# RWKV-7 trunk: state kept in PSUM and updated on 64x64 quarters, with scores, state and outputs sharing two banks

## The chip, the cores and the metric

The kernel runs on 1 core of one Trainium2 chip. The metric is device time in microseconds (us) of one execution; lower is better. Names: TensorE (PE, weight loads PEld), VectorE (DVE), ScalarE (ACT), GpSimd (POOL), SyncE (SP, which issues most loads).

## The reference, cut to what matters

One layer on 2048 tokens of width 1024, float32: RMSNorm, RWKV-7 time mixing, residual, RMSNorm, squared-ReLU MLP, residual, final RMSNorm. The time mixing has 16 heads of 64 and a 64x64 state per head:

```python
def rwkv7_step(state, inp):
    r_t, w_t, k_t, v_t, a_t, b_t = inp
    sa = jnp.einsum('bhvk,bhk->bhv', state, a_t)
    state = (state * w_t[:, :, None, :]
             + sa[..., None] * b_t[:, :, None, :]
             + v_t[..., None] * k_t[:, :, None, :])
    y = jnp.einsum('bhvk,bhk->bhv', state, r_t)
    return state, y
```

Here a is minus the normalized key direction and b is it times a learned rate. Afterwards y is normalized per head, given a bonus term, gated, and multiplied by an output matrix.

## The kernel before

**Tiling of the recurrence.** The sequence is cut into 4 blocks of 512 tokens, each block into 4 windows of 128 tokens (w = 0 to 15), each window into 4 chunks of 32 tokens (c = 0 to 3). Decays are folded into the factors per window, so within a window the state only gains terms, and the window's total decay is multiplied on at its last chunk. The 16 heads go as 8 even and 8 odd heads (`par` 0 and 1); head p of a parity is written p = 4 hf + k.

**One window**, in the order in which `stage_b` issues it:

- `b_pre` loads the factors (`Le`, `Lo`: those of the even heads on partitions 0 to 63 and of the odd heads on 64 to 127; `Bk`: both), and makes the scores for two chunks at a time: `sce` from `Le` in the PSUM bank tagged `pre`, `sco` from `Lo` in the bank tagged `chain`, by 64x64 matmuls in four positions of the array (line 589). ScalarE copies the part for the solve (line 593), VectorE masks the scores into the other halves of `Le` and `Lo` (line 595).
- `b_solve` inverts the 32x32 unit triangles by forward substitution on VectorE (lines 604 to 612); `b_inv` spreads the inverse into `xbd`.
- `b_chain` issues `b_chunk` four times. A chunk: transposes of `Bk` through `pre` into `ls` (tile `pb`, every second chunk); `pw` (line 652), its copy `ws` (line 655), the pseudo values `pu` = `xbd` times `ws` (line 658), four copies of `pu` into the rows of `suv` (lines 659 to 662), the new state `pS` (lines 665 and 666), and its copies into the state rows of the next `suv` (line 672, or line 670 with the decay at c = 3). `suv` holds, per parity, 64 rows of state, 32 of pseudo values and 32 of v; `ls` holds a 64x64 identity on the state's rows, so that `pS` is the whole state, old plus new.
- `b_y` multiplies the window's outputs y from `Lo`, `Le` and the four `suv` into the banks `y0` and `y1` (line 688).
- `b_fin` normalizes and gates y on VectorE and ScalarE one parity after the other (lines 704 to 722), transposes the result through `y0` or `y1` (tile `pz`, line 726) and copies it to `zt` (line 727). It is called one window late: behind the chain of window w + 1.

**Order around it.** The program's instructions are issued by a list scheduler; the order in which the code issues them is their priority. The recurrence of a block is a generator, `side`, of 80 steps, that the main work draws from at a set rate. From about 676 to 1045 us block 0 runs beside the projections of later blocks (`v_proj`, `g_proj`, matmuls `pv`, `pg`, `pm`); there the loads of the next window are double buffered and its scores come ahead of the chain. From then on `phase_c` computes the output projection (`po`), the MLP (`pu` with lines 90 to 92, `pd`) and the norms of block i while block i + 1 recurs, and draws what is left of the side stage before the next block's output projection (`"complete"`). Its matmuls are splits of float32 into two fp32r parts, three products each (lines 90 to 92); ScalarE makes the first part of each weight tile (line 84), VectorE the rest (line 85). The norms' broadcasts use `y0`.

PSUM has 8 banks: `pre`, `chain`, `y0`, `y1`, and four for the main work's matmuls.

Of the kernel before, what the change touches and what calls it, by code (L numbers as in the profile page):

```python
# [9 lines left out]
F32 = mybir.dt.float32  # L10
F32R = mybir.dt.float32r
AF = mybir.ActivationFunctionType
ALU = mybir.AluOpType
# [4 lines left out]
P = 128  # L18
# [6 lines left out]
NB = T // TB  # L25
# [3 lines left out]
NC = WIN // CH  # L29
# [10 lines left out]
def trunk(ctx: ExitStack, tc, xt, vecs, lnw, lnb, wr, wk, wv, w1a1, w2, a2,  # L40
          g1m, g1t, g2m, g2t, wo, up, down, outT):
    nc = tc.nc
# [456 lines left out]
    start = head(0)  # L499
# [58 lines left out]
    CB = 1  # L558
# [7 lines left out]
    def b_pre(w, r, bp, ps, cfg):  # L566

        i, wd = divmod(w, NWB)
        Le = bp.tile([P, 8, NC, 64], F32, tag="Le", name=f"Le{w}", bufs=cfg["l"])
        Lo = bp.tile([P, 8, NC, 64], F32, tag="Lo", name=f"Lo{w}", bufs=cfg["l"])  # L570
        bk = bp.tile([P, 8, NC, 64], F32, tag="Bk", name=f"Bk{w}", bufs=cfg["l"])
        ec = bp.tile([P, KT], F32, tag="ecw", name=f"ecw{w}", bufs=cfg["l"])
        bon = bp.tile([P, 16], F32, tag="bonw", name=f"bonw{w}", bufs=2)
        nc.sync.dma_start(Le[0:64], d_ar[i][wd, 0:64])
        nc.sync.dma_start(Lo[64:128], d_ar[i][wd, 64:128])
        nc.sync.dma_start(bk, d_bk[i][wd])
        nc.sync.dma_start(ec, d_ec[i][:, :, wd])
        nc.sync.dma_start(bon, d_bon[i][:, wd, :])

        sy = bp.tile([P, 8, NC, 32], F32, tag="sys", name=f"sy{w}")  # L580
        for c in range(0, NC, 2):

            sce = ps.tile([P, 2, 4, 64], F32, tag="pre", name=f"sce{w}_{c}", bufs=cfg["pre"])
            sco = ps.tile([P, 2, 4, 64], F32, tag="chain", name=f"sco{w}_{c}", bufs=CB)
            for e2 in range(2):
                for k in range(4):
                    for (sc, L, rw, hf, cl) in ((sce, Le, 0, 0, 64), (sco, Lo, 64, 0, 0), (sce, Le, 0, 1, 0), (sco, Lo, 64, 1, 64)):
                        p, rr = 4 * hf + k, slice(rw, rw + 64)
                        nc.tensor.matmul(sc[cl:cl + 64, e2, k, :], bk[rr, p, c + e2, :], L[rr, p, c + e2, :],
                                         start=(e2 + k == 0), stop=True, skip_group_check=True, tile_position=(rw, cl))  # L590
            c2 = slice(c, c + 2)
            for n, sc in enumerate((sce, sco)):
                nc.scalar.copy(sy[0:96, 4 * n:4 * n + 4, c2, :].rearrange("s p c t -> s c p t"), sc[0:96, :, :, 0:32])
            for (sc, L, cl, hf, to) in ((sce, Le, 64, 0, 64), (sce, Le, 0, 1, 64), (sco, Lo, 0, 0, 0), (sco, Lo, 64, 1, 0)):
                nc.vector.tensor_tensor(L[to:to + 64, 4 * hf:4 * hf + 4, c2, :].rearrange("s p c t -> s c p t"), sc[cl:cl + 64],
                                        mask[cl:cl + 64].unsqueeze(1).unsqueeze(1).to_broadcast((64, 2, 4, 64)), ALU.mult)
            yield
            yield
        r.Le, r.Lo, r.bk, r.ec, r.bon, r.sy = Le, Lo, bk, ec, bon, sy
# [27 lines left out]
    def b_chunk(w, c, r, bp, ps, cfg):  # L627
# [27 lines left out]
        nc.vector.tensor_copy(ws, pw)  # L655
        pu = ps.tile([P, 4, 64], F32, tag="chain", name=f"pu{w}_{c}", bufs=CB)
        for k in range(4):
            nc.tensor.matmul(pu[:, k, :], xbd[:, k, c, :], ws[:, k, :], start=(k == 0), stop=True, skip_group_check=True)  # L658
        nc.vector.tensor_copy(S[0][64:96, 0:4], pu[64:96])
        nc.vector.tensor_copy(S[0][64:96, 4:8], pu[0:32])  # L660
        nc.scalar.copy(S[1][0:32, 0:4], pu[32:64])
        nc.scalar.copy(S[1][0:32, 4:8], pu[96:128])  # L662
        pS = ps.tile([P, 8, 64], F32, tag="chain", name=f"pS{w}_{c}", bufs=CB)
        for p in range(8):
            nc.tensor.matmul(pS[0:64, p, :], lsc[0][:, p, :], S[0][:, p, :], start=(p == 0), stop=True, skip_group_check=True)  # L665
            nc.tensor.matmul(pS[64:128, p, :], lsc[1][:, p, :], S[1][:, p, :], start=(p == 0), stop=True, skip_group_check=True)
        for par in range(2):
            r = slice(64 * par, 64 * par + 64)
            if c == NC - 1:
                nc.vector.tensor_tensor(Sn[par][r], pS[r], ec[r].unsqueeze(2).to_broadcast((64, 8, 64)), ALU.mult)  # L670
            else:
                nc.scalar.copy(Sn[par][r], pS[r])

    def b_chain(w, r, bp, ps, cfg):

# [4 lines left out]

    def b_y(w, r, ps):

        r.y = []
        for par, L in ((0, r.Le), (1, r.Lo)):
            y = ps.tile([P, 8, 64], F32, tag=f"y{par}", name=f"y{w}_{par}")
            for p in range(8):
                for c in range(NC):
                    nc.tensor.matmul(y[32 * c:32 * c + 32, p, :], L[:, p, c, 32:64], suv[(w * NC + c) % NS][par][:, p, :],
                                     start=(p == 0), stop=True, skip_group_check=True, tile_position=(0, 32 * c))
            r.y.append(y)  # L690

    def b_fin(w, r, bp, ps, cfg):

# [6 lines left out]
        for par, y in enumerate(r.y):  # L700
# [19 lines left out]
            nc.vector.tensor_mul(yc, yc, lnwb[:, cols].rearrange("p (h v) -> p h v", v=64))  # L720
            nc.vector.tensor_add(yc, yc, vb)
            nc.vector.tensor_mul(yc, yc, gb)
            pz = ps.tile([P, 4, P], F32, tag=f"y{par}", name=f"pz{w}_{par}")
            ycf = yc.rearrange("p h v -> p (h v)")
            for k in range(4):
                nc.tensor.transpose(pz[:, k, :], ycf[:, k * P:k * P + P], ident)
# [2 lines left out]

    def stage_b(i, bp, ps, cfg):  # L730
        w0, w1 = i * NWB, (i + 1) * NWB
        r, last = Win(), None
        yield from b_pre(w0, r, bp, ps, cfg)
        yield from b_solve(w0, r, bp)
        for w in range(w0, w1):
            b_inv(w, bp)
            for _ in range(cfg["slack"]):
                yield
            nxt = Win()
            early = cfg["l"] > 1 and w + 1 < w1  # L740
            if early:
                yield from b_pre(w + 1, nxt, bp, ps, cfg)
            yield from b_chain(w, r, bp, ps, cfg)
            if last:
                yield from b_fin(w - 1, last, bp, ps, cfg)
            b_y(w, r, ps)
            if w + 1 < w1:
                if not early:
                    yield from b_pre(w + 1, nxt, bp, ps, cfg)
                yield from b_solve(w + 1, nxt, bp)  # L750
            last, r = r, nxt
        yield from b_fin(w1 - 1, last, bp, ps, cfg)


    p0 = ExitStack()
# [62 lines left out]
    def c_norm(i):  # L818

        h = hs[i]  # L820
        ns = nss.setdefault(i, [])
        pb = norm(h, f"n{i}", cp, psb, "y0", 2)
        rb = cp.tile([P, TB], F32, tag="rb", name=f"nB{i}")
        nc.scalar.copy(rb, pb)
        rbs[i] = rb
        if i > 0:
            for k in range(KT):
                n32 = cp.tile([P, TB], F32, tag="t0", name=f"hn{i}_{k}", bufs=2)
                nc.vector.scalar_tensor_tensor(n32, h[k], vec[:, V_FFN, k:k + 1], rb, ALU.mult, ALU.mult)
                ns.append(split(e, n32, f"hn{i}_{k}"))  # L830
# [30 lines left out]

    def c_sum(i):

        return norm_sum(hs[i], f"f{i}", cp, psb, "y0", 2, 1, i == NB - 1)

    def c_final(i, so):
        h = hs[i]
        pb = norm_rest(so, f"f{i}", cp, psb, "y0")
        rb = cp.tile([P, TB], F32, tag="rb", name=f"fB{i}")
        nc.scalar.copy(rb, pb)  # L870
        for k in range(KT):
# [120 lines left out]
```

## Time and profile before

| | |
|---|---|
| median of 3 runs | 2978.05 us (2973.08 to 2983.74) |
| the profiled execution | 2975.33 us |
| its span, first to last instruction | 2973.6 us |
| mean granted TensorE clock | 0.976 of full speed |

The profile is one execution. A timeline row gives an instruction's start and duration in us, its engine, source line, output and inputs, and shape; a matmul's duration contains its way through the array, so the distance from one start to the next is what a matmul occupies. A float32 matmul of the recurrence is listed as two instructions. Merged rows carry a count (x64). In brackets is the engine's idle time before the instruction and what ended it. A few records of matmuls can be missing.

### The profile page before, as it was taken

Reading aid. Unit: us, or ns where it says so; the run is one execution under the profiler, and the core shown is the slowest. Engines: PE = TensorE matmul, PEld = TensorE weight load, DVE = VectorE, ACT = ScalarE, POOL = GpSimd, SP = SyncE. Lnnn points to the kernel's source line nnn. Section 1 sums busy time; section 2 is a strip of 40 time slices with the busy share of each in tenths; the row PEclk is TensorE's granted clock in tenths of the full one; section 3 lists DMA queues with packets and bytes.
Section 4 is the critical chain, followed back from the end, with each engine's and each line's share of the span. In section 5 each row is a group of like instructions: output and inputs, shape, how many; then the busy total and the mean of one; then the engine's idle time right before and its main releaser. Section 6 shows DMA issues by size and latency. Waiting matters only on the chain.

```text
span 2973.6 us, 49932 instructions
## 1 busy us (share of the span) xinstructions
PE 2809.7 (94%) x19144; PEld 2126.0 (71%) x19144; DVE 2062.6 (69%) x3882; ACT 1423.2 (48%) x2607; POOL 238.2 (8%) x316
## 2 busy tenths in 40 slices
PE   8999999987989989999999999999999999999998
PEld 5766667754555667777777777778777777878886
DVE  5688888867886667678668767865886696544443
ACT  5667666743564243443434454353445435443342
POOL 0102020120010100000012000001200000110000
PEclk9999999998999999999999999999999999999999
DMA  4444454565553533424343333443343342333332
GB/s 132 153 152 163 153 184 160 170 203 188 166 177 125 156 95 94 114 83 122 97 144 110 109 113 88 116 118 118 111 114 107 96 112 83 113 122 97 91 100 78
DMA packets 192542, 373.91 MB, mean 126 GB/s; under 512 B 41136, under 2 KB 41712, under 8 KB 187696
## 3 DMA queue, kind: packets, MB, share of 16 engines
q1 hardware_dynamic: 175216, 305.49, 35.0%
q0 software_dynamic: 17088, 65.24, 5.8%
q8 instruction: 150, 2.46, 0.4%
q14 instruction: 88, 0.72, 0.1%
HBM read 303.32 MB, written 67.32 MB: 125 GB/s over the span
## 4 chain that ended last, share of the span: by engine, by line
PE 46%; DVE 11%; ACT 3%; DMA 3%; issue 2%; POOL 1%; SPq 0%; DVEq 0%; ACTq 0%; POOLq 0%
PE pd L92 6%; PE pd L90 6%; PE pd L91 6%; PE pu L90 5%; PE pu L91 5%; PE pu L92 5%; DVE tmp L611 2%; DVE M L612 2%; PE po L90 2%; PE po L91 2%; PE po L92 2%; PE pS L665 1%; PE pu L658 1%; DMA Le<-d_ar 1%; DVE d_wl L85 1%
## 5 line engine op out<-in xcount | busy, mean ns | idle before, releaser
L92 PE MATMUL pd<-uh,d_wl 128*128 128x512 f32 x1024 | 408.1, 399 | 8.8 <-DVE d_wl L85 8.6
L90 PE MATMUL pd<-uh,d_wh 128*128 128x512 f32 x1024 | 407.1, 398 | 2.4 <-ACT d_wh L84 2.4
L91 PE MATMUL pd<-ul,d_wh 128*128 128x512 f32 x1024 | 402.1, 393 | 0.0
L84 ACT CAST d_wh<-d_w 128x512 fp32r<-128x512 f32 x256 | 158.0, 621 | 353.5 <-PE pd L91 161.4
L84 ACT CAST u_wh<-u_w 128x512 fp32r<-128x512 f32 x256 | 157.8, 620 | 317.7 <-PE pd L91 114.3
L860 DVE TENSOR_TENSOR h<-h,pd 128x512 f32<-128x512 f32 x256 | 174.6, 682 | 154.6 <-PE pd L92 153.8
L85 DVE TENSOR_TENSOR d_wl<-d_w,d_wh 128x512 fp32r<-128x512 f32 x256 | 178.0, 698 | 107.5 <-ACT d_wh L84 97.6
L92 PEld LDWEIGHTS pd<-uh,d_wl 128*128 128x128 f32 x1024 | 192.9, 188 | 61.5 <-DVE d_wl L85 18.7
L85 DVE TENSOR_TENSOR u_wl<-u_w,u_wh 128x512 fp32r<-128x512 f32 x256 | 181.0, 710 | 78.5 <-ACT u_wh L84 69.7
L90 PEld LDWEIGHTS pd<-uh,d_wh 128*128 128x128 f32 x1024 | 193.5, 189 | 42.0 <-ACT d_wh L84 3.2
L91 PEld LDWEIGHTS pd<-ul,d_wh 128*128 128x128 f32 x1024 | 193.0, 189 | 42.3 <-DVE ul L849 0.2
L611 DVE TENSOR_TENSOR tmp<-M 96x30 f32<-96x30 f32 (+14 forms) x480 | 156.9, 327 | 18.9 <-POOL M L605 9.3
L612 DVE TENSOR_TENSOR M<-M,tmp 96x30 f32<-96x30 f32 (+14 forms) x480 | 161.1, 336 | 10.5
L849 DVE TENSOR_TENSOR ul<-rl,uh 128x512 fp32r<-128x512 f32 x128 | 90.2, 705 | 67.9 <-ACT uh L848 67.5
L194 PE MATMUL pv<-v,xv 128*128 128x512 f32 x256 | 124.8, 623 | 11.6 <-DMA v<-in_wv 9.7
L845 ACT ACTIVATE rl<-rl 128x512 f32<-128x512 f32 x128 | 80.9, 632 | 39.8 <-DVE rl L842 37.2
L665 PEld LDWEIGHTS pS<-suv,ls 128*64 128x64 f32 x1024 | 64.6, 138 | 34.0 <-ACT suv L662 29.7
L194 PEld LDWEIGHTS pv<-v,xv 128*128 128x128 f32 x256 | 46.7, 196 | 58.1 <-issue 40.2
L848 ACT CAST uh<-rl 128x512 fp32r<-128x512 f32 x128 | 79.3, 620 | 3.6
L658 PEld LDWEIGHTS pu<-ws,xbd 128*128 128x128 f32 x512 | 64.9, 193 | 22.3 <-DVE ws L655 9.7
L665 PE MATMUL pS<-suv,ls 128*64 128x64 f32 x1024 | 73.7, 225 | 6.5 <-ACT suv L662 6.0
L605 POOL TENSOR_SCALAR_AFFINE_SELECT M<-M 96x1024 f32<-96x1024 f32 x16 | 23.0, 1438 | 700.6 <-DVE M L604 700.6
(711 smaller groups left out, 7074.7 us busy)
## 6 DMA issues: line engine op xcount, KB each, us to landing
u_w<-in_up SPq DMA_DIRECT2D x256, 256.0 KB, 2.7
d_w<-in_down SPq DMA_DIRECT2D x256, 256.0 KB, 2.6
k_w<-in_wk SPq DMA_DIRECT2D x64, 256.0 KB, 2.7
r_w<-in_wr SPq DMA_DIRECT2D x64, 256.0 KB, 2.7
d_ar<-ar POOLq DMA_DIRECT2D x32, 512.0 KB, 3.2
d_bk<-bk POOLq DMA_DIRECT2D x32, 512.0 KB, 3.4
Bk<-d_bk SPq DMA_DIRECT2D x16, 1024.0 KB, 5.0
o_w<-in_wo SPq DMA_DIRECT2D x64, 256.0 KB, 2.9
```

Of the source, the lines that this page charges most:

```text
L84: nc.scalar.copy(hi[0:rows, 0:cols], raw[0:rows, 0:cols])
L85: nc.vector.tensor_tensor(lo[0:rows, 0:cols], raw[0:rows, 0:cols], hi[0:rows, 0:cols], ALU.subtract)
L90: nc.tensor.matmul(out, lhs[0], rhs[0], start=first, stop=False)
L91: nc.tensor.matmul(out, lhs[0], rhs[1], start=False, stop=False)
L92: nc.tensor.matmul(out, lhs[1], rhs[0], start=False, stop=last)
L194: nc.tensor.matmul(pv[tt], xs_[k][:, c], w, start=(k == 0), stop=(k == KT - 1))
L611: nc.vector.tensor_tensor(tv, M[0:96, s + 1:32, s:s + 1].to_broadcast((96, n, s)), M[0:96, s:s + 1, 0:s].to_broadcast((96, n, s)), ALU.mult)
L612: nc.vector.tensor_tensor(M[0:96, s + 1:32, 0:s], M[0:96, s + 1:32, 0:s], tv, ALU.add)
L658: nc.tensor.matmul(pu[:, k, :], xbd[:, k, c, :], ws[:, k, :], start=(k == 0), stop=True, skip_group_check=True)
L665: nc.tensor.matmul(pS[0:64, p, :], lsc[0][:, p, :], S[0][:, p, :], start=(p == 0), stop=True, skip_group_check=True)
L849: nc.vector.tensor_tensor(ul, rl, uh, ALU.subtract)
L860: nc.vector.tensor_add(h[m], h[m], pd)
```

## The change

- The scores `sce` and `sco` become the two halves of one tile of two banks, tag `st`.
- `pu` is multiplied in two column halves of 64 instead of 128 columns at once.
- The state isn't built anew in each chunk: it stays in a tile of two banks (tag `st` again, one per window), which the first chunk writes in full (128 rows, identity included) and chunks 1 to 3 add to, by matmuls over the 64 rows of pseudo values and v alone. Each matmul has a 64x64 position: parity 0 takes rows 64 to 127 of the array and parity 1 rows 0 to 63, parity and head half hf give the column half, and each parity has its own bank.
- The state leaves PSUM in four pieces of 64x256 instead of two of 64x512.
- The two outputs y become one tile of two banks, tag `st`; `pz` and the norms' tiles go to tag `pre`. So `st` holds in turn scores, state, y.
- `b_fin` of window w follows `b_y` of window w directly, ahead of the next window's `b_pre` (in block 0, where that comes early, ahead of the next `b_solve`).

```diff
         for c in range(0, NC, 2):
-            sce = ps.tile([P, 2, 4, 64], F32, tag="pre", name=f"sce{w}_{c}", bufs=cfg["pre"])
-            sco = ps.tile([P, 2, 4, 64], F32, tag="chain", name=f"sco{w}_{c}", bufs=CB)
+            sct = ps.tile([P, 2, 2, 4, 64], F32, tag="st", name=f"sc{w}_{c}")
+            sce, sco = sct[:, 0], sct[:, 1]
...
         for k in range(4):
-            nc.tensor.matmul(pu[:, k, :], xbd[:, k, c, :], ws[:, k, :], start=(k == 0), stop=True, skip_group_check=True)
+            for cl in (0, 64):
+                nc.tensor.matmul(pu[cl:cl + 64, k, :], xbd[:, k, c, cl:cl + 64], ws[:, k, :], start=(k == 0), stop=True,
+                                 skip_group_check=True, tile_position=(0, cl))
...
-        pS = ps.tile([P, 8, 64], F32, tag="chain", name=f"pS{w}_{c}", bufs=CB)
-        for p in range(8):
-            nc.tensor.matmul(pS[0:64, p, :], lsc[0][:, p, :], S[0][:, p, :], start=(p == 0), stop=True, skip_group_check=True)
-            nc.tensor.matmul(pS[64:128, p, :], lsc[1][:, p, :], S[1][:, p, :], start=(p == 0), stop=True, skip_group_check=True)
-        for par in range(2):
-            r = slice(64 * par, 64 * par + 64)
+        if c == 0:
+            r.st = ps.tile([P, 2, 8, 64], F32, tag="st", name=f"st{w}")
+        for k in range(4):
+            for par, hf, cl in ((0, 0, 0), (1, 0, 64), (0, 1, 64), (1, 1, 0)):
+                p = 4 * hf + k
+                r0 = 0 if c == 0 else 64 - 64 * par
+                rw = slice(0, P) if c == 0 else slice(r0, r0 + 64)
+                nc.tensor.matmul(r.st[cl:cl + 64, par, k, :], lsc[par][rw, p, :], S[par][rw, p, :], start=(c == 0 and k == 0), stop=True,
+                                 skip_group_check=True, tile_position=(r0, cl))
+        for par, hf, cl in ((0, 0, 0), (1, 0, 64), (0, 1, 64), (1, 1, 0)):
+            rw = slice(64 * par, 64 * par + 64)
+            ph = slice(4 * hf, 4 * hf + 4)
+            src = r.st[cl:cl + 64, par, 0:4, :]
             if c == NC - 1:
-                nc.vector.tensor_tensor(Sn[par][r], pS[r], ec[r].unsqueeze(2).to_broadcast((64, 8, 64)), ALU.mult)
+                nc.vector.tensor_tensor(Sn[par][rw, ph], src, ec[rw, ph].unsqueeze(2).to_broadcast((64, 4, 64)), ALU.mult)
             else:
-                nc.scalar.copy(Sn[par][r], pS[r])
+                nc.scalar.copy(Sn[par][rw, ph], src)
...
-        r.y = []
+        yt = ps.tile([P, 2, 8, 64], F32, tag="st", name=f"y{w}")
+        r.y = [yt[:, 0], yt[:, 1]]
...
-            pz = ps.tile([P, 4, P], F32, tag=f"y{par}", name=f"pz{w}_{par}")
+            pz = ps.tile([P, 4, P], F32, tag="pre", name=f"pz{w}_{par}")
...
             yield from b_chain(w, r, bp, ps, cfg)
-            if last:
-                yield from b_fin(w - 1, last, bp, ps, cfg)
             b_y(w, r, ps)
+            yield from b_fin(w, r, bp, ps, cfg)
             if w + 1 < w1:
...
-            last, r = r, nxt
-        yield from b_fin(w1 - 1, last, bp, ps, cfg)
+            r = nxt
...
-        pb = norm(h, f"n{i}", cp, psb, "y0", 2)
+        pb = norm(h, f"n{i}", cp, psb, "pre", 2)
```

## Rows read from the trace of the kernel before

**Rows 1.** The page's first part: busy us (share of the span) and instructions.
```profile
PE 2809.7 (94%) x19144; PEld 2126.0 (71%) x19144; DVE 2062.6 (69%) x3882; ACT 1423.2 (48%) x2607; POOL 238.2 (8%) x316
```

**Rows 2.** Busy us of PE, PEld, DVE, ACT, POOL by stretch; clock, DMA, GB/s.
```profile
676.00:1045.00 369.00, 327.66 (x3072) 198.23 (x3071) 280.44 (x595) 173.41 (x338) 39.94 (x62) 0.94 0.52 159
1045.00:2510.00 1465.00, 1409.28 (x11592) 1124.65 (x11593) 1055.44 (x2055) 643.23 (x1235) 69.14 (x70) 0.99 0.37 108
```

**Rows 3.** Waits of TensorE, 1045 to 2510 us: total, times, longest.
```profile
PE pd L92 <- DVE d_wl L85: 8.6, 12, 1.5
```

**Rows 4.** Timeline of TensorE, one chunk: start us, duration us, instruction.
```profile
1320.72 0.40 PE L90 MATMUL pu<-hn_6h,u_wh 128*128 128x512 f32 x1
1321.05 0.24 PE L652 MATMUL pw<-suv,Le 128*32 128x64 f32 x1
...
1321.97 0.39 PE L92 MATMUL pu<-hn_6h,u_wl 128*128 128x512 f32 x1
1322.20 0.40 PE L90 MATMUL pu<-hn_7h,u_wh 128*128 128x512 f32 x1
1322.43 1.00 PE L658 MATMUL pu<-ws,xbd 128*128 128x64 f32 x8
...
1323.56 0.39 PE L92 MATMUL pu<-hn_7h,u_wl 128*128 128x512 f32 x1
...
1324.94 0.40 PE L92 MATMUL pd<-uh,d_wl 128*128 128x512 f32 x1
1325.27 0.27 PE L665 MATMUL pS<-suv,ls 128*64 128x64 f32 x1
...
1326.68 0.40 PE L91 MATMUL pd<-ul,d_wh 128*128 128x512 f32 x1
```

**Rows 5.** Timeline of TensorE, a joined score run; 63 of its instructions left out.
```profile
1121.25 0.39 PE L92 MATMUL pd<-uh,d_wl 128*128 128x512 f32 x1
1121.57 0.27 PE L589 MATMUL sce<-Le,Bk 64*64 64x64 f32 x1
...
1123.01 0.40 PE L91 MATMUL pd<-ul,d_wh 128*128 128x512 f32 x1
```

**Rows 6.** Timeline of TensorE, a pair of score runs apart.
```profile
1238.78 1.15 PE L589 MATMUL sce<-Le,Bk 64*64 64x64 f32 x32 [0.80 <-DMA Le<-d_ar]
...
1242.03 0.40 PE L91 MATMUL pd<-ul,d_wh 128*128 128x512 f32 x1
1242.36 1.15 PE L589 MATMUL sco<-Lo,Bk 64*64 64x64 f32 x32
...
1243.78 0.39 PE L90 MATMUL pd<-uh,d_wh 128*128 128x512 f32 x1
```

**Rows 7.** Groups by line and form: busy us, mean ns, idle before.
```profile
L672 ACT COPY suv<-pS 64x512 f32<-64x512 f32 x96 | 55.7, 581 | 34.3 <-PE pS L666 33.4
...
L647 ACT COPY ls<-pb 64x256 f32<-64x256 f32 x128 | 46.8, 366 | 30.1 <-PE pb L643 22.1 <-PE pS L666 6.0
```

**Rows 8.** Timelines of TensorE and VectorE around y, windows 5 and 7.
```profile
1231.43 1.10 PE L688 MATMUL y<-suv,Le 128*32 128x64 f32 x64
...
1478.29 1.39 DVE L670 TENSOR_TENSOR suv<-pS,ecw 64x512 f32<-64x512 f32 x2 [0.21 <-PE pS L666]
...
1482.93 1.10 PE L688 MATMUL y<-suv,Le 128*32 128x64 f32 x64
...
1487.71 1.10 PE L688 MATMUL y<-suv,Lo 128*32 128x64 f32 x64
...
1499.45 0.69 DVE L715 TENSOR_REDUCE st<-y 128x8 f32<-128x512 f32 x1
```

**Rows 9.** Timelines of ScalarE and TensorE at the end of block 2.
```profile
2003.91 0.59 ACT L727 COPY zt<-pz 128x512 f32<-128x512 f32 x1
...
2013.57 0.59 ACT L727 COPY zt<-pz 128x512 f32<-128x512 f32 x1 [4.05 <-PE pz L726]
...
2018.20 0.40 PE L90 MATMUL po<-z_0h,o_wh 128*128 128x512 f32 x1
```

More of the change, by code (lines that the diff above doesn't have):

```diff
@@ L681, in b_y @@
     def b_y(w, r, ps):
-        r.y = []
+        yt = ps.tile([P, 2, 8, 64], F32, tag="st", name=f"y{w}")
+        r.y = [yt[:, 0], yt[:, 1]]
         for par, L in ((0, r.Le), (1, r.Lo)):
-            y = ps.tile([P, 8, 64], F32, tag=f"y{par}", name=f"y{w}_{par}")
             for p in range(8):
                 for c in range(NC):
-                    nc.tensor.matmul(y[32 * c:32 * c + 32, p, :], L[:, p, c, 32:64], suv[(w * NC + c) % NS][par][:, p, :],
+                    nc.tensor.matmul(r.y[par][32 * c:32 * c + 32, p, :], L[:, p, c, 32:64], suv[(w * NC + c) % NS][par][:, p, :],
                                      start=(p == 0), stop=True, skip_group_check=True, tile_position=(0, 32 * c))
-            r.y.append(y)
     def b_fin(w, r, bp, ps, cfg):
@@ L731, in stage_b @@
         w0, w1 = i * NWB, (i + 1) * NWB
-        r, last = Win(), None
+        r = Win()
         yield from b_pre(w0, r, bp, ps, cfg)
@@ L862, in c_sum @@
     def c_sum(i):
-        return norm_sum(hs[i], f"f{i}", cp, psb, "y0", 2, 1, i == NB - 1)
+        return norm_sum(hs[i], f"f{i}", cp, psb, "pre", 2, 1, i == NB - 1)
     def c_final(i, so):
         h = hs[i]
-        pb = norm_rest(so, f"f{i}", cp, psb, "y0")
+        pb = norm_rest(so, f"f{i}", cp, psb, "pre")
         rb = cp.tile([P, TB], F32, tag="rb", name=f"fB{i}")
```

## The prediction

> **What bounds the kernel now.** I read the page's first part, then a table by stage, then the waits of TensorE, then timelines of single chunks. TensorE is busy for 94% of the span [rows 1], and by stage that is 328 of 369 us in the stretch in which the recurrence of block 0 runs beside value and gate projections (676 to 1045 us), and 1409 of 1465 us where the recurrences of blocks 1 to 3 run beside the output projection and the MLP (1045 to 2510 us) [rows 2]. The rest of the span holds nothing of the change. In the long stretch the largest wait of TensorE for one thing comes to 8.6 us [rows 3]: the recurrence is cheap there in latency, because independent MLP matmuls fill in, and dear in TensorE slots, because each of its instructions displaces one of theirs. So the question is how long a run of recurrence matmuls keeps the MLP stream off TensorE. I price a run by the stream around it: from the last stream matmul before the run to the second one after it, less two stream steps of 0.23 us (1321.97 to 1322.20 in rows 4). That counts what a change of form costs on entering and leaving.
>
> **The state update.** Now it is 16 matmuls a chunk, 128 rows by 64 columns, which the profile lists as 32 instructions: 1324.94 to 1326.68 is 1.74 us, less 0.46 gives 1.28 us [rows 4]. Two column halves start together, so these are 16 steps. After the change 48 of the 64 chunks (those that aren't a window's first) use 64x64 quarters, whose four positions can start together: 8 steps. Quarters stand in the trace already, in the scores. Where all four run, 64 instructions cost 1121.25 to 1123.01, 1.76 less 0.46, 1.30 us [rows 5], for twice as many instructions as the state's. Eight steps are seen in the `pw` run, 32 instructions in four column quarters: 1320.72 to 1321.97, 1.25 less 0.46, 0.79 us [rows 4]. I take 0.79, so 0.49 us saved for each of 48 chunks, 23.5 us: 17.6 in the long stretch (36 chunks), 5.9 in the first (12). The other end is no gain: where only two positions are in flight, 32 quarter instructions cost as much as the state does now (1.29 us, next but one paragraph). I take the upper end because the new order visits the four positions in turn, as the scores in rows 5 do, with each row half on its own bank. A window's first chunk keeps its 16 steps and costs what it does.
>
> **Pseudo values in column halves.** 4 matmuls of 128x128 (8 instructions) cost 1322.20 to 1323.56, 1.36 less 0.46, 0.90 us [rows 4]. In halves they are 16 instructions in pairs, 8 steps, by the `pw` run 0.79 us: 0.11 us saved for each of 64 chunks, 7.0 us (5.3 and 1.8). Ends: if the halves didn't overlap, 16 steps at the state's 1.28 us would lose 0.38 us a chunk, 24 us; the state's own pairs, two halves of 64 columns starting together, are the same form and speak against that.
>
> The stream's step grows from 0.23 to 0.33 us on entering the `pw` and `pS` runs, and stays 0.23 us on entering the full-size `pu` run [rows 4]. The Trainium skill (TensorEngine Tiling (Array Packing), Key Properties) says that changing the tiling mode drains TensorE, which speaks against halving `pu`: the trace agrees by that 0.10 us. By the rule alone, two switches more in 64 chunks would lose about 13 us where I forecast a gain of 7; by the rows, the 0.79 us has both switches in it.
>
> **Scores.** Now the even heads' scores take the bank `pre` and the odd ones `chain`, each issued as its inputs come; after, both stand in one tile, so neither starts before the tile is free. Where they run apart, each 32 instructions cost a full run: 1242.03 to 1243.78, 1.75 less 0.46, 1.29 us [rows 6], so 2.58 us a pair against 1.30 joined. Of the 22 pairs of score runs in the long stretch I count 16 apart, as at 1238.78 and 1242.36. What separates them is the odd heads' load, queued behind the even heads'. After the change the tile is freed by the window's last read of y, some 17 us after the y matmuls began (rivals), while the loads leave when those matmuls end, so both should lie there. 16 times 1.28 is 20.5 us; in five windows two runs stand back to back and already share an entry and an exit, for which I take off 0.5 us each (an estimate): 18 us. The first stretch has two pairs apart: 2.5 us. The lower end is nothing, if they stay apart.
>
> **Copies.** The state leaves PSUM in four copies of 64x256 instead of two of 64x512: 4 times 366 ns less 2 times 581 ns [rows 7] is 0.30 us more on ScalarE in 48 chunks, 14.6 us; I take as much again per window for the same split of VectorE's products at a window's end, 16 times 0.3 us. ScalarE is busy 643 and VectorE 1055 of 1465 us [rows 2], and MLP matmuls cover the chunk's latency; without that cover it would be up to 20 us. But each chunk's own path gets shorter by 0.49 and 0.11 and longer by 0.30 us, so I count nothing.
>
> **Finishing moved.** Normalizing window w now stands after chain w+1; after, right behind y of w, before the scores of w+1. The work is the same. Its four loads a window now come ahead of the next window's five on SP's queue, and the second half's two wait for the first half's buffers, which puts what is behind them up to 10 us back (the halves' distance, 2003.91 to 2013.57 in rows 9); y holds the scores' tile longer than that anyway. y itself now waits for the state's last products, about 1.5 us (four short copies). Each block's last chain is issued two of its 80 side steps later (its first chunk at the 75th instead of the 73rd, counted in the code), 12 us at 1465/3/80, about 6 us a step. In return one window's finishing, two halves of about 10 us of which it shares VectorE with the chain, leaves the block's tail; I take 1 us late per block, 3 us, with 0 and 12 us a block as ends. Transposes and norm broadcasts move to the bank `pre`; they meet only `pb` there, with stream matmuls to fill in: nothing.
>
> **Sum.** Long stretch 17.6 + 5.3 + 18 = 40.9 us. TensorE was busy in 96% of it, but the stream's weights are split on VectorE, 72% busy and already waited for [rows 2, 3]; I take 85%, 34.8 us. First stretch 5.9 + 1.8 + 2.5 = 10.2 us; TensorE is idle in 11% there and the recurrence sets its own pace, so half, 5.1 us. Less 3: 36.9 us. From the profiled execution's 2975.3 us that is 2938.4; it lies 2.7 us below the median, so **2941 us** on the median.
>
> **Rivals.**
> *The shared banks hold the recurrence up (slower).* Scores of the next window now follow y by 7.4 us (1231.43 to 1238.78, rows 6 and 8). After, they wait for y's last read in the finishing: 1482.93 to 1500.14 is 17.2 us in today's order [rows 8]. 9.8 us in three windows of a block is 30 us; the output projection starts 4 us after the block's last z [rows 9], so 26 us a block would show, 77 us in three: 2978 + 77 - 37 = 3018 us. It decides from about 16 us of delay a block, where 12 eat the gain and 4 the margin. Against it: the finishing of the window before, which puts y's second half 9.4 us behind the state's last product today (1478.29 to 1487.71), no longer stands there. The Trainium skill (PSUM — Partial Sum Buffer, Summary: rules for kernel authors) advises prompt evacuation, which is this rival's side; no row shows two tenants of one bank waiting so long. 12%.
> *Only part of the packing comes.* Quarters run in pairs: no state gain, 23.3 us at 85% plus 2.2 less 3, 19 us, 2959 us. Scores stay apart: 22.9 at 85% plus 3.9 less 3, 20 us, 2958 us. Together 16%.
> *Freed slots stay empty,* because the split weights set the pace: 5.1 less 3, 2976 us. VectorE at 72% and a wait of 8.6 in 1465 us speak against it. 8%.
> *As forecast,* 64%.
>
> **How the numbers follow.** The likeliest case spans 2924 (all 51 us gained, and 3 for the runs' spread of some 5 us to each side) to 2957 us (60% of the long stretch, nothing in the first, 3 us late). With the partial packing and its spread the range is 2923 to 2968 us and leaves out about 2 in 10. A change of 0.3%, 9 us, is about what a measurement of this kernel can tell from none. Faster by more: 64 + 16 = 80%; within: 8%; slower: 12%.
>
> **What would show it.** Right: a state run near 0.8 us in the same account in the chunks after a window's first, `pu` at 0.8, scores always 64 together, the long stretch some 35 us shorter at the same granted clock, and z no later before the output projection. Wrong: quarters in pairs, the stream waiting for split weights, or waits of scores for y's reads with idle TensorE ahead of each output projection.

## The result and the profile after

The changed kernel takes 2993.35 us (median of 5 runs, 2991.95 to 3004.57) against 2978.05 us before (5 runs, 2972.97 to 2983.74): ratio 1.0066, 95% interval 1.0048 to 1.0085 (over all runs, not of the two medians). The forecast was 2941 us, so the change is slower where I expected faster. The profiled execution spans 2991.1 us; the granted clock is 0.975 (0.976 before).

The first part of the page, and the table by stretch in the order of [rows 1, 2]:

```profile
PE 2809.8 (94%) x19656; PEld 2072.4 (69%) x19656; DVE 2064.8 (69%) x3914; ACT 1432.9 (48%) x2701; POOL 239.7 (8%) x316
```
```profile
676.00:1045.00 369.00, 315.11 (x3184) 175.85 (x3183) 274.06 (x574) 171.49 (x358) 39.95 (x61) 0.94 0.52 159
1045.00:2510.00 1465.00, 1404.03 (x11676) 1082.94 (x11676) 1056.59 (x2093) 643.82 (x1284) 70.21 (x70) 0.99 0.37 107
```

TensorE is as busy in the long stretch as before (1404 against 1409 us), with less done: the first output product of block 3 comes at 2550.1 instead of 2534.4 us. The loss isn't spread. Of the 17.5 us of the span, 6.6 are there when block 0's norm sum is multiplied (1067.2 against 1060.6), 19.3 at block 1's first output product (1517.1 against 1497.8), and from there to block 3's 3.6 come back. The waits of TensorE from 1045 to 2510 us [rows 3]:

```profile
PE pz L737 <- DVE yc L733: 12.8, 14, 4.1
PE pu L92 <- DVE u_wl L85: 6.8, 4, 3.0
PE pd L92 <- DVE d_wl L85: 6.7, 11, 0.8
```

**One chunk after** (timeline of TensorE, a window's second chunk, to hold against [rows 4]), and beneath it the copies on VectorE and ScalarE that feed it:

```profile
1346.23 0.40 PE L92 MATMUL pd<-uh,d_wl 128*128 128x512 f32 x1
1346.56 0.69 PE L659 MATMUL pu<-ws,xbd 128*64 128x64 f32 x16
1347.18 0.50 PE L90 MATMUL pd<-uh,d_wh 128*128 128x512 f32 x1
1347.52 0.40 PE L91 MATMUL pd<-ul,d_wh 128*128 128x512 f32 x1
1347.75 0.39 PE L92 MATMUL pd<-uh,d_wl 128*128 128x512 f32 x1
1348.07 0.33 PE L675 MATMUL st<-suv,ls 64*64 64x64 f32 x2
1348.33 0.50 PE L90 MATMUL pd<-uh,d_wh 128*128 128x512 f32 x1
1348.67 0.40 PE L91 MATMUL pd<-ul,d_wh 128*128 128x512 f32 x1
1348.90 0.39 PE L92 MATMUL pd<-uh,d_wl 128*128 128x512 f32 x1
1349.23 0.33 PE L675 MATMUL st<-suv,ls 64*64 64x64 f32 x4
1349.49 0.50 PE L90 MATMUL pd<-uh,d_wh 128*128 128x512 f32 x1
1349.92 0.68 PE L675 MATMUL st<-suv,ls 64*64 64x64 f32 x26
1350.52 0.50 PE L91 MATMUL pd<-ul,d_wh 128*128 128x512 f32 x1
1350.87 0.39 PE L92 MATMUL pd<-uh,d_wl 128*128 128x512 f32 x1
```
```profile
1347.29 0.42 DVE L661 COPY suv<-pu 32x256 f32<-32x256 f32 x1 [1.09 <-PE pu L659]
1347.75 0.42 DVE L662 COPY suv<-pu 32x256 f32<-32x256 f32 x1
```
```profile
1348.25 0.36 ACT L663 COPY suv<-pu 32x256 f32<-32x256 f32 x1 [3.20 <-DVE suv L662]
1348.64 0.37 ACT L664 COPY suv<-pu 32x256 f32<-32x256 f32 x1
1350.63 1.51 ACT L684 COPY suv<-st 64x256 f32<-64x256 f32 x4 [1.62 <-PE st L675]
```

The state's 32 listed instructions are no longer one run. They come as 2, 4 and 26, with MLP matmuls between. The four copies of `pu` end one after another (1347.71, 1348.17, 1348.61, 1349.01), and each piece goes, in the order of issue, as far as the first matmul whose copy isn't done: one matmul behind the first copy, two behind the third, the other 13 behind the fourth. All 48 runs behind 1068 us are cut so, each with a last piece of 26. In the forecast's account, 1347.75 to 1348.67 less 0.46 is 0.46 us, and 1348.90 to 1350.87 less three steps of 0.23 is 1.28 us: 1.74 us a chunk, where 0.79 was forecast and 1.28 stood before. The 26 alone take 0.60 us: the quarters run as fast as priced, and the cutting takes it back. A window's first chunk is cut too (at 1340.51, 1341.66 and 1342.47 us), and costs 2.21 us by the same account, where I had left it at 1.28.

**Scores** (timeline of TensorE, ends of one run of 64, as [rows 5]), and the **state copies** (group by form, as [rows 7]):

```profile
1128.24 0.40 PE L92 MATMUL pd<-uh,d_wl 128*128 128x512 f32 x1
1128.57 0.27 PE L589 MATMUL sc<-Le,Bk 64*64 64x64 f32 x1
...
1130.00 0.39 PE L91 MATMUL pd<-ul,d_wh 128*128 128x512 f32 x1
```
```profile
L684 ACT COPY suv<-st 64x256 f32<-64x256 f32 x192 | 70.3, 366 | 37.3 <-PE st L675 34.9
```

A joined run costs 1.76 less 0.46, 1.30 us, as forecast, and 21 of the 22 runs behind 1068 us are whole; the copies take the 366 ns that was taken from [rows 7].

**A table for all that follows.** From 1068 us on I take each distance between neighbouring MLP or output-projection matmuls, less 0.229 us, and put it down to the kinds of matmuls that stand between the two, in equal shares; "none" is where nothing stands between. Not all kinds are listed. The last three rows split "all kinds" in another way: time in which no matmul was in flight; of the other time half of what was at a granted clock of 0.50; and the rest, which is what TensorE's slots cost. It is worked out from the records, in us, one execution each (E5's and E11's profiled executions are 5 us above their medians):

| | before | after | E1 | E2 | E4 | E5 | E8 | E9 | E11 |
|---|---|---|---|---|---|---|---|---|---|
| state | 63.5 | 80.9 | 46.2 | 70.3 | 63.0 | 44.5 | 66.6 | 69.0 | 58.8 |
| scores | 54.1 | 27.8 | 28.6 | 27.9 | 34.1 | 28.2 | 41.1 | 29.7 | 28.8 |
| `pu` | 46.6 | 37.5 | 38.1 | 35.5 | 44.1 | 35.9 | 41.8 | 35.2 | 35.0 |
| `pw` | 33.0 | 48.1 | 54.0 | 37.1 | 33.0 | 46.6 | 33.8 | 34.4 | 45.7 |
| `pz` | 16.3 | 26.7 | 29.6 | 24.8 | 16.4 | 27.6 | 17.5 | 25.5 | 27.2 |
| y | 25.7 | 26.1 | 27.7 | 28.5 | 25.7 | 32.4 | 28.6 | 29.0 | 24.8 |
| none | 54.9 | 58.5 | 58.5 | 40.4 | 54.0 | 56.4 | 38.8 | 43.5 | 42.3 |
| all kinds | 352.8 | 366.7 | 343.4 | 324.3 | 327.8 | 331.1 | 329.1 | 328.9 | 322.2 |
| TensorE idle | 55.8 | 59.3 | 71.1 | 57.6 | 55.9 | 74.2 | 47.5 | 57.4 | 62.5 |
| lower clock | 18.4 | 17.7 | 22.8 | 13.0 | 12.9 | 21.6 | 11.1 | 13.1 | 13.2 |
| slots | 278.6 | 289.7 | 249.4 | 253.7 | 259.0 | 235.4 | 270.5 | 258.4 | 246.5 |

**Block 0.** The issue of loads by SyncE around the end of block 0's recurrence, after, and under it the same before (timelines; rows of other loads left out):

```profile
978.47 0.79 SPq L636 DMA_DIRECT2D suv<-d_v  x2
...
995.43 0.45 SPq L574 DMA_DIRECT2D Le<-d_ar  x1
996.23 0.81 SPq L81 DMA_DIRECT2D o_w<-in_wo  x2
```
```profile
955.54 0.79 SPq L636 DMA_DIRECT2D suv<-d_v  x2
...
973.29 0.45 SPq L574 DMA_DIRECT2D Le<-d_ar  x1
```

And what TensorE and SyncE waited for there, after (views of waits, 676 to 1068 us and, the last row, 960 to 1004 us):

```profile
PE po L90 <- DMA o_w<-in_wo: 6.2, 1, 6.2
```
```profile
SPq L636 <- PE y L700: 17.8, 1, 17.8
```

Scores, state and y take turns in one tile, so window 3's y can't be begun before its state has left: all 128 instructions of y stand together at 977.36 us, where before the first ones stood among the chain's matmuls and the last run began at 955.04. The v rows of the next window (line 636) overwrite what y reads, so they wait 17.8 us for it on SyncE's queue, and behind them the loads of window 4 leave at 995.4 instead of 973.3 us. The output weights stand behind those; TensorE is idle 6.2 us for them. Against the kernel before only 0.4 us are lost up to there: its own weights left at 996.45, and its first output product came at 1001.2 us (1001.6 after), behind waits of 3.1 and 2.6 us. What is late is block 1's recurrence: window 4's scores come at 1009.3 instead of 991.2 us, and the 6.6 and 19.3 us above arise behind that. That is my slower rival's mechanism, tenants of one tile waiting for each other, at a place that I had not looked at.

### The profile page after: what moved, and what is told of

It is laid out like the page before. It is cut to its first block, busy times and chain, and to the rows that moved or that the text cites. A ratio compares the mean times of both kernels' runs of the same rounds, so it can differ in the third digit from the quotient of the medians.

```text
span 2991.1 us, 51097 instructions
## 1 busy us (share of the span) xinstructions
PE 2809.8 (94%) x19656; PEld 2072.4 (69%) x19656; DVE 2064.8 (69%) x3914; ACT 1432.9 (48%) x2701; POOL 239.7 (8%) x316
## 4 chain that ended last, share of the span: by engine, by line
PE 66%; DVE 15%; issue 8%; ACT 5%; DMA 4%; POOL 2%; SPq 0%; DVEq 0%; POOLq 0%; ACTq 0%
PE pu L92 6%; PE pu L91 6%; PE pu L90 6%; PE pd L90 6%; PE pd L92 6%; PE pd L91 5%; DVE M L612 2%; PE pk L90 2%; PE pk L91 2%; DVE tmp L611 2%; PE pk L92 2%; PE st L675 2%; PE po L90 2%; PE po L92 2%; PE po L91 2%
## 5 line engine op out<-in xcount | busy, mean ns | idle before, releaser
L675 PEld LDWEIGHTS st<-suv,ls 64*64 64x64 f32 (+1 forms) x2048 | 64.4, 135 | 74.0 <-DVE suv L661 20.8
L854 ACT ACTIVATE rl<-rl 128x512 f32<-128x512 f32 x128 | 80.9, 632 | 39.3 <-DVE rl L851 36.5
L675 PE MATMUL st<-suv,ls 64*64 64x64 f32 (+1 forms) x2048 | 89.0, 230 | 6.3 <-ACT suv L663 3.6
L684 ACT COPY suv<-st 64x256 f32<-64x256 f32 x192 | 70.3, 366 | 37.3 <-PE st L675 34.9
```

The costliest lines, as they stand in the source:

```text
L675: nc.tensor.matmul(r.st[cl:cl + 64, par, k, :], lsc[par][rw, p, :], S[par][rw, p, :], start=(c == 0 and k == 0), stop=True, skip_group_che ...
L854: nc.scalar.activation(rl, rl, AF.Square)
```

## The experiments

Ratios are to the kernel before on the same chip, with their 95% intervals; I turn them into us at 2978.

### First round: which part costs

**E1, the state's run gathered.** The changed kernel; the state's other 15 matmuls are issued only behind the one whose operand is copied last.

```diff
-            for par, hf, cl in ((0, 0, 0), (1, 0, 64), (0, 1, 64), (1, 1, 0)):
+            for par, hf, cl in ((1, 1, 0), (0, 0, 0), (1, 0, 64), (0, 1, 64)):
...
-                nc.tensor.matmul(r.st[cl:cl + 64, par, k, :], ...
+                with behind(lead):
+                    mm = nc.tensor.matmul(r.st[cl:cl + 64, par, k, :], ...
+                lead = lead or mm
```

> The changed kernel, with the state's 16 matmuls of a chunk issued as one run, behind the one whose input is copied last. Theory 1 (pieces): the loss is that the scheduler cuts this run into pieces of 2, 4 and 26 instructions, each of which costs an entry into and an exit from the MLP stream; as one run the state costs about 0.8 us a chunk (1.29 in a window's first) in place of 1.65, which is 35 us less between 1045 and 2510 us and a few before: 2950 to 2962 us. Theory 2 (shared banks): the loss is the recurrence waiting for the shared tile and ending late in each block; the order of the state's matmuls changes nothing of that: 2985 us or more. Theory 3 (quarters): the 64x64 form itself is dear; as one run it costs no less than the 1.29 us of before: 2985 us or more.

2970.27 us, 0.9973 (0.9961 to 0.9985), 28 us below the changed kernel by the ratios, where 31 to 43 were expected. The timeline shows the run whole:

```profile
1344.45 0.39 PE L92 MATMUL pd<-uh,d_wl 128*128 128x512 f32 x1
1344.77 0.69 PE L680 MATMUL st<-suv,ls 64*64 64x64 f32 x32
1345.39 0.51 PE L90 MATMUL pd<-uh,d_wh 128*128 128x512 f32 x1
1345.73 0.40 PE L91 MATMUL pd<-ul,d_wh 128*128 128x512 f32 x1
```

1.28 less 0.46 is 0.82 us, so the forecast's 0.79 holds for a run that stays whole. The pieces are about half of the 57 us between forecast and result. In the table 40 us of slots come free; TensorE stands idle 12 us longer, and the lower clock costs 5 more.

**E2, the state rebuilt whole.** The changed kernel with the state as before (16 matmuls into the bank `chain`, two copies); scores, y, `pu` and finishing as changed.

```diff
-        if c == 0:
-            r.st = ps.tile([P, 2, 8, 64], F32, tag="st", name=f"st{w}")
...
+        pS = ps.tile([P, 8, 64], F32, tag="chain", name=f"pS{w}_{c}", bufs=CB)
```

> The changed kernel, with the state rebuilt whole in each chunk in the bank of the pseudo values, as before; the rest of the change stays. Theory 1: the new tile in that bank can't be issued before the bank's four copies are done, so the run is whole again at 1.29 us a chunk: some 19 us less than the changed kernel, about 2974 us. Theory 2: scores, y and finishing are shared as in the changed kernel, so it stays at 2985 us or more. Theory 3: about 2974 us too.

2945.25 us, 0.9895 (0.9878 to 0.9912). Everything but the state gains 31 us; the state in PSUM costs 51, where the theories had 19 at most. The run is whole here, as theory 1 says: the code gives `chain` one buffer, so `pS` can't be had there before all four copies of `pu` are done. By that reading the allocation had kept the run together before, and the tile kept over the chunks took it away.

**E3, `pw` gathered as well.** E1, with `pw`'s matmuls behind the one whose operand comes last.

```diff
-            for (L, Sx, q, p) in ((Le, S[0], 0, 4 + k), (Lo, S[1], 1, k), (Le, S[0], 2, k), (Lo, S[1], 3, 4 + k)):
+            for (L, Sx, q, p) in ((Lo, S[1], 3, 4 + k), (Le, S[0], 0, 4 + k), (Lo, S[1], 1, k), (Le, S[0], 2, k)):
...
+                with behind(lead):
```

> The first experiment with the run of pw gated in the same way, behind the one that needs the state's last copy. Theory 1: pw, which costs 61 us with its neighbours between 1045 and 2510 us against 49 before, gets some of that back: 5 to 8 us less than the first experiment. Theories 2 and 3: the same as the first experiment within 3 us.

2963.21 us, 0.995 (0.9934 to 0.9966): 7 us more. `pw` was cut in turn (9 of its 48 runs behind 1068 us in E1), since the state now comes in four copies; gathered, it takes 47.8 us where it took 54.0 in E1, which is still 15 more than before.

**E4, scores alone.** The kernel before; the even heads' scores are issued behind the first of the odd heads'.

```diff
-                    for (sc, L, rw, hf, cl) in ((sce, Le, 0, 0, 64), (sco, Lo, 64, 0, 0), ...
+                    for (sc, L, rw, hf, cl) in ((sco, Lo, 64, 0, 0), (sce, Le, 0, 0, 64), ...
...
+                        with behind(lead):
```

> The kernel before, with nothing changed but the order of the scores' matmuls: the even heads' are issued behind the first of the odd heads', so the four positions always run together. By the prediction's price of 1.28 us for each of 16 pairs of score runs that were apart, less what adjoining runs already share, about 18 us less between 1045 and 2510 us and 2 before: 2958 us. If joining the scores only moves the wait elsewhere: 2973 to 2983 us.

2951.95 us, 0.9913 (0.9889 to 0.9938). Joining alone is worth 26 us, more than the 20.5 that were forecast for both stretches, and 1 to 1: scores, `pu` and all kinds fall by 20, 2.5 and 25 us in the table, of which 5.5 are the lower clock.

### Second round: block 0, the copies, the finishing

**E5, block 0's state as before.** E3 with the rebuilt state in block 0 and the state in PSUM in blocks 1 to 3.

```diff
+        if i == 0:
+            pS = ps.tile([P, 8, 64], F32, tag="chain", name=f"pS{w}_{c}", bufs=CB)
...
+        else:
```

> The third experiment (state run and pw each in one piece), with block 0's state rebuilt whole in the bank of the pseudo values, as before; blocks 1 to 3 keep it in PSUM. Theory 4 (tenancy in block 0): block 0 has the next window's scores ahead of the chain, so there the one tile passes from scores to state to y to the finishing and back, and each chain waits for the finishing before it; that makes the first norm of the output stretch some 6 us late and block 1 later still. Then this kernel loses both: 2946 to 2954 us, with that norm at 1058 to 1061 us. If block 0 is not the place: 2960 to 2966 us.

2946.82 us, 0.9907 (0.9888 to 0.9925): 13 us below E3, from one block, with its first output product at 994.8 us (1001.6 after). But it only equals E2, though the state takes 26 us less of the stream there. The table says where that went: the slots cost 18 us less than in E2, but TensorE is idle 17 us longer, and the lower clock costs 9 more.

**E6, the four copies shared by two engines.** E5, with the even heads' state copied by VectorE.

```diff
-                nc.scalar.copy(Sn[par][rw, ph], src)
+                (nc.scalar.copy if par else nc.vector.tensor_copy)(Sn[par][rw, ph], src)
```

> The fifth experiment, with the state's four copies shared between VectorE (even heads) and ScalarE (odd heads) in chunks 1 to 3 of blocks 1 to 3. Theory 5 (four copies): four copies one after another on ScalarE bring the next pw's operands later than the two did, and TensorE waits inside pw's run, about 4 us a block; two engines end that: 8 to 14 us less than the fifth experiment. If the copies are hidden: the same within 3 us, or a little more for VectorE's work.

2956.83 us, 0.9941 (0.9922 to 0.9959): 10 us slower than E5. `pw` waits less for the state's copies, as theory 5 had it (9.5 us in E5), but the wait for the split weights, which VectorE makes, grows from 5.5 us (waits of TensorE, 1068 to 2500 us):

```profile
PE pd L92 <- DVE d_wl L85: 13.4, 9, 3.5
...
PE pw L657 <- ACT suv L705: 5.1, 10, 0.6
```

The 10 us are what the clock took: the mean granted clock is 0.971 or 0.972 in all four executions, against 0.972 to 0.977 in E5's, and its shortfall times the span is on average 83.5 us against 73.6. Two of the added stretches at 0.50 stand right behind waits for split weights of 3.3 and 3.5 us (to 1722.3 and 2232.8). So this edit can't tell what the four copies in a row cost: it shortened one wait and lengthened others, and the clock fell behind those.

**E7, four copies with the rebuilt state.** E2, each copy of 64x512 cut into two of 64x256.

```diff
-                nc.scalar.copy(Sn[par][rw], pS[rw])
+                for hf in range(2):
+                    nc.scalar.copy(Sn[par][rw, 4 * hf:4 * hf + 4], pS[rw, 4 * hf:4 * hf + 4])
```

> The second experiment (state rebuilt whole, 2945 us), with its two ScalarE copies of 64x512 cut into four of 64x256; nothing else. Theory 5: pw waits as in the changed kernel, 8 to 16 us more, 2953 to 2961 us. If the copies are hidden: 2943 to 2948 us.

2945.67 us, 0.9899 (0.988 to 0.9919), the same as E2. The 0.30 us a chunk are hidden, as the forecast counted them.

**E8, the finishing moved alone.** The kernel before, with `b_fin` right behind `b_y`.

```diff
-            if last:
-                yield from b_fin(w - 1, last, bp, ps, cfg)
             b_y(w, r, ps)
+            yield from b_fin(w, r, bp, ps, cfg)
```

> The kernel before, with nothing changed but the place of the finishing: window w is finished right behind its y, while scores, state and y keep banks of their own. If moving the finishing is what makes the recurrence late (theory 2 without the shared tile): 2985 us or more, with idle TensorE ahead of the output projections. Theory 4: without the shared tile the move costs little, 2970 to 2984 us.

2954.18 us, 0.9928 (0.991 to 0.9947), a gain of 21 us where I had forecast a loss of 3. The waits of TensorE, 1045 to 2510 us (in [rows 3] the first was 8.6):

```profile
PE pd L92 <- DVE d_wl L85: 3.9, 4, 1.9
...
PE pz L726 <- DVE yc L722: 3.6, 7, 1.7
```

"None" falls by 16 us and scores by 13, though nothing joins them by order. Of the 24 us in all kinds, TensorE's idle time has 8, the lower clock 7 and the slots 8. The wait for split weights is 4.7 us less; that VectorE held them up while it normalized beside the next chain fits that row, but the row holds only a part of the gain, and what else the move changes isn't shown.

### Third round: do the gains add, and is block 0 by itself

**E9, own banks.** The kernel before with E4's order, E8's move and `pu` in halves; no shared tile.

> The kernel before with three parts of the change and none of the shared tile: scores joined by order, pseudo values in column halves, the finishing right behind y; scores, state and y keep the banks that they had. Theory (what is left of the gain is independent of the shared tile, and the tile only costs): the gains measured apart add up in part, 26 us of the joined scores, 20 us of the finishing, 5 us of the halves; each alone already takes part of the same idle and stream time, so I expect 2930 us (2922 to 2942), below the 2945 us of the changed kernel with the state rebuilt whole. Rival (the shared tile costs nothing once the state is out of it): 2945 us, the same as that kernel, because the two differ only in the banks.

2955.03 us, 0.9935 (0.992 to 0.9949). Both expectations fall: the gains of E4 (26) and E8 (21) don't add at all, and the shared tile, without the state in it, is 12 us better by the ratios than separate banks (10 by the medians; the two also join the scores in different ways, by the tile and by order). In the table E8 and E4 take partly the same time from the scores (41.1 and 34.1, together 29.7), and what E9 saves over E8 there and in `pu` (18 us) returns in `pz` (8.0), "none" (4.7) and others. Of the 8.3 us between the profiled spans of E9 and E2, 5.5 lie ahead of the first output product (1005.6 against 1000.0).

**E10, block 0 alone.** The changed kernel with block 0's state rebuilt, the pieces left as they are.

```diff
+        if i == 0:
+            pS = ps.tile([P, 8, 64], F32, tag="chain", name=f"pS{w}_{c}", bufs=CB)
...
+        else:
```

> The changed kernel with only block 0's state rebuilt whole per chunk in the chain's bank; blocks 1 to 3 keep the state in PSUM, in pieces as issued. Theory (two separate costs, the pieces and the tile's tenancy in block 0): the first stretch gains what the run with both state runs gathered gained from the same edit, 16 us, and some 2 us of pieces there, so 2974 us (2968 to 2980), the end of window 3's last chain product back near 961 us from 976, and the pieces of 2, 4 and 26 instructions still there behind 1068 us. Rival (pieces alone, block 0 as dear as any other quarter of the recurrence): a fifth of the 23 us, 2988 us, and the mark stays near 976.

2978.11 us, 1.0015 (1.0004 to 1.0026): 15 us back, as 13 in the pair E3 and E5, where no state run is cut, so the two costs are separate. SyncE's loads (timeline) leave where they did before, and the first output product comes 5.0 us earlier than after (4.6 earlier than before), without the 6.2 us:

```profile
973.22 0.45 SPq L574 DMA_DIRECT2D Le<-d_ar  x1
```
```profile
996.59 0.50 PE L90 MATMUL po<-z_0h,o_wh 128*128 128x512 f32 x1 [1.51 <-ACT o_wh L84]
```

The delay of block 0 builds up over its four windows. Their first state matmuls start at 747.7, 811.5, 887.9 and 948.3 us in the changed kernel and at 743.5, 801.6, 873.8 and 932.9 here. In the first three the shared tile makes the state follow the scores ahead of it by 5.7 to 6.8 us, where it is 1.1 to 1.8 with the state in `chain`; and y begins some 5 us behind the start of the state's last run, where here what is left of y follows by 1 us.

### Fourth round: do freed slots still count

**E11, short run without a kept tile.** E2, but in chunks 1 to 3 of blocks 1 to 3 the quarters take the new rows alone, into a fresh tile; the old state isn't added, so its sum is left out.

```diff
+        if i and c:
+            pS = ps.tile([P, 4, 64], F32, tag="chain", name=f"pS{w}_{c}", bufs=CB)
+            pT = ps.tile([P, 4, 64], F32, tag="pre", name=f"pT{w}_{c}")
...
+                    rw = slice(64 - 64 * par, 128 - 64 * par)
+                    with behind(lead):
+                        mm = nc.tensor.matmul((pT if par else pS)[cl:cl + 64, k, :], ...
```

> The changed kernel with the state rebuilt whole in the chain's bank (2945 us), except in chunks 1 to 3 of the windows of blocks 1 to 3: there the 64x64 quarters run over the 64 new rows alone, gathered in one run, into a fresh tile per chunk (the chain's bank and the one tagged pre), and the four copies take that alone. The state of the chunk before is left out, so its sum is not built. So TensorE gets the quarters' short run and no tile is kept over chunks. Theory 6 (freed TensorE slots no longer bind the kernel at 2945 us: VectorE's split weights and the finishing do): the state's excess in the long stretch falls from 70 to about 45 us, waits and stream excess take it up, and the time is 2945 us within 6. Rival (the slots still bind, and it is the wait on the tile kept over chunks that takes them back in the other kernels): 85% of the 25 us, 2924 us.

2940.83 us, 0.9893 (0.9875 to 0.9912), by the ratios equal to E2 (0.9895). The run is short; it begins here and the stream goes on 0.62 us later:

```profile
1345.30 0.39 PE L91 MATMUL pu<-hn_3l,u_wh 128*128 128x512 f32 x1
1345.62 0.27 PE L679 MATMUL pT<-suv,ls 64*64 64x64 f32 x1
```

State and y together (they stand side by side here) take 15 us less than in E2, where 25 were expected of the state alone; `pw` takes 8.6 more, `pz` 2.4. All slots together are 7 us less, and TensorE is idle 5 us longer. So the shorter state run brought no time that can be measured, but it freed too little to decide: 85% of 7 us is 6, which the interval of 5.5 us to each side doesn't tell from nothing.

## Why the prediction was wrong, point by point

**The step that failed: "The state update ... I take 0.79".** The 0.79 us was read from a `pw` run and put on 16 matmuls that would be issued together. It is right for a run (0.82 in E1), but nothing in the changed code makes them one: they came as three pieces and cost 1.74 us. Before, by the code and E2, the tile's allocation made them one; with a tile kept over the window each matmul is free as soon as its own copy, and those of the matmuls issued ahead of it, are done. I compared forms and not what releases each instruction, though the copies' order stands in the code. In the long stretch this makes 36 times 0.95 plus 12 times 0.93 us, 45 us of slots by the two prices; 37 by the table (80.9 against 43.8, which is 36 times 0.79 and 12 times 1.28). Of the time, E1 gets 28 us back and E3 7 more, since `pw` was cut as well, which the forecast had no term for.

The rule of the Trainium skill that a change of tiling mode drains TensorE (TensorEngine Tiling (Array Packing), Key Properties) agrees with what a piece pays: the stream's step is 0.32 to 0.33 us going in and 0.34 or 0.35 us coming out (0.43 us between two pieces with one stream matmul between them), where it is 0.23 us elsewhere, and three pieces pay it three times.

**The slower rival was real, in block 0, and its place was wrong.** I looked for it at the ends of blocks 1 to 3, where scores wait for y's last read, and priced 26 us a block. There it costs nothing that shows. The end of block 2 after, to hold against [rows 9] (timelines of TensorE and of ScalarE):

```profile
2015.20 1.08 PE L700 MATMUL y<-suv,Lo 128*32 128x64 f32 x64
...
2025.45 0.60 PE L737 MATMUL pz<-ident,yc 128*128 128x128 f32 x4
...
2032.31 0.39 PE L90 MATMUL po<-z_0h,o_wh 128*128 128x512 f32 x1
```
```profile
2026.09 0.59 ACT L738 COPY zt<-pz 128x512 f32<-128x512 f32 x1 [2.93 <-PE pz L737]
2036.28 0.59 ACT L738 COPY zt<-pz 128x512 f32<-128x512 f32 x1 [4.06 <-PE pz L737]
```

The output projection starts 17 us behind y and even ahead of the second half of z, without a gap. Blocks 2 and 3 take 515.3 and 517.8 us from one first output product to the next, before 520.4 and 516.2. It costs 15 us once (E10), where block 0's state waits for the scores, y for the state, and y holds up SyncE's loads for block 1. "The first stretch, half" counted gains alone and had no term for it.

**Finishing moved, "I take 1 us late per block": sign wrong.** Alone it gains 21 us (E8). I counted queue places and steps, and nothing of what the normalizing displaces where it stood. Transposes put at "nothing": `pz` takes 10 us more (16.3 to 26.7), but 25.5 in E9 too, with `pz` in its old banks, so the bank isn't why; the cause is open.

**Scores: right, somewhat low.** 26 us alone, forecast 20.5. **`pu` in halves:** 1346.23 to 1347.52 less 0.46 is 0.83 us, forecast 0.79, before 0.90; 4.5 us of slots for 7.0. **Copies counted as nothing:** right (E7).

**"I take 85%":** wrong as one factor for all terms. E4 gave its saving 1 to 1; E9 gave nothing more on top of others, and in E5 18 us of freed slots came back as idle time and lower clock. So the rival "freed slots stay empty" holds in part, though not for the first 30 us, and VectorE's split weights, its reason, aren't what TensorE waits longer for in E5 (its view has 5.5 us for them, E2's 5.2).

**Sum.** By the ratios: the change +20 us; pieces of the state out, -8 (E1); `pw` gathered, -15 (E3); block 0 apart, -28 (E5). That this is near the forecast's -37 is luck: E2 has -31 without any change of the state, and a gain of the finishing is in both that the forecast didn't have.

**Open.** Why a state run that is 0.5 us shorter brings nothing in blocks 1 to 3 is shown only as far as where the time goes: idle TensorE and the lower clock. In E5 `pw` waits for the state's copies, and in E2 the state waits as long for those of `pu` (views of waits, 1068 to 2500 us, E5 and E2):

```profile
PE pw L657 <- ACT suv L705: 9.5, 15, 1.0
```
```profile
PE pS L669 <- ACT suv L664: 9.3, 23, 1.3
```

So that row by itself isn't the difference; several waits, each a few us longer in E5, are. In E11 "none" is only 2 us above E2, and `pw` is as dear as in E5. E7 speaks against the number of copies by itself, with the rebuilt state; E6 doesn't settle it. The order in which the list scheduler lays the runs is a candidate; it wasn't isolated.

Nor was the difference between E2 and E9 traced beyond block 0. No version beat E2 by more than the runs can tell; among those that build the whole state, E2, E5 and E7 are equal, 28 to 31 us faster than the kernel before.

## What to carry to other kernels

Before pricing a packed run, ask what holds its instructions together: list the release of each one's operands, and if a scheduler may place them singly, count an entry and an exit for every group of operands that comes at its own time, or gather the run behind its last operand. A PSUM tile that is kept longer takes away a wait that may have been keeping order, and makes its tenants queue; follow that wait to the loads behind it on the issuing queue, above all at the border between two stages. Gains that free the same engine need not add; measure the parts alone and together, and look at that engine's idle time and granted clock before counting a freed slot as time.

## What was not expected of the hardware

Ahead of the first output product TensorE's granted clock falls to the lower of its two levels. One stretch after, one before and two in E10 (busy by stretch; the granted clock is the third number from the end):

```profile
994.50:1004.60 10.10, 3.87 (x11) 2.84 (x11) 6.27 (x10) 6.02 (x11) 0.00 (x0) 0.50 0.88 219
```
```profile
997.30:1007.50 10.20, 7.57 (x39) 5.69 (x36) 9.17 (x15) 5.65 (x13) 0.00 (x0) 0.50 0.92 287
```
```profile
992.10:995.40 3.30, 2.97 (x90) 2.62 (x90) 2.99 (x5) 3.30 (x7) 0.00 (x0) 0.50 0.71 241
996.60:1004.00 7.40, 7.09 (x30) 5.54 (x31) 5.54 (x10) 2.35 (x6) 0.00 (x0) 1.00 0.86 280
```

After, it is 0.50, or 1.2 GHz, behind a wait of 4.05 us (to 994.34) and stays so through the wait of 6.23 us (to 1001.60); the first output matmuls start 0.43 us apart. Before, it is 0.50 behind a wait of 3.12 us (to 995.46) and through one of 2.63 us. In E10 it is 0.50 behind a wait of 3.46 us (to 990.58) and 1.00 again when the output products start, behind one of 1.51 us. So a gap there costs more than its own length, in both kernels, and the loss of the change isn't from this: before and after have some 10 us at 0.50 there.

Copies from one PSUM bank went one after another, though VectorE and ScalarE took two each: ScalarE's two began at 1348.25, 0.08 us behind VectorE's last, after 3.20 us of idle time put down to it. That is an order of the program, which the profile reads from its semaphores; no run here shows that the chip needs it.
